# Feed-forward of a hybrid layer on one core: pools of their own for operands, weights and results, and the last pair's products stored by other queues

## The chip, the cores and the metric

The kernel runs on 1 core of one Trainium2 chip. The metric is the device time of one execution in microseconds (us), the median of the runs shown; lower is better. PE is TensorE, DVE VectorE, ACT ScalarE, POOL GpSimd, SP SyncE (it only issues transfers here); SPq is SP's queue of transfers.

## The reference

One layer: RMSNorm and an input projection, a Mamba-2 scan and differential attention side by side, an output projection, and the feed-forward, which is the part that matters here. All of it is float32, 1024 tokens by 1024 channels, with a feed-forward width of 2816.

```python
    x = x + jnp.concatenate([y_ssd, y_att], axis=-1) @ w_out[l]
    h = rms_norm(x, norm2_w[l])
    x = x + (jax.nn.silu(h @ w_gate[l]) * (h @ w_up[l])) @ w_down[l]
```

## The kernel before

Every float32 product is made of three matmuls (`mm3`, L168 to L170): each operand is split into a high part (a cast on ACT, L156) and a low remainder (a subtraction on DVE or POOL, L157).

**Gate and up.** The 2816 columns are 22 tiles `f` of 128. The first two go the plain way; the other 20 go through `GateUp`, one step per `f`, in which a 2x2 block scheme replaces eight block products by seven (`PRODUCTS`: a11, s2, s1, s3, a12, s4, a22, in this order). The activations' seven operands of four tiles each (`ops`) are made once and stay in SBUF, 16 KB a partition for each, seven in all; product `j` of each step reads only operand `PRODUCTS[j]`. A step is 7 x 4 x 3 = 84 matmuls into four PSUM banks a to d. The weights of a step come as four raw tiles `wr`, POOL makes four differences `t` of them (L1164), and ACT and DVE split the seven into `op`; `run` prepares step n+1 while step n multiplies. The result of step `f` is `m`, finished on DVE (L1216, L1233, L1238).

**The store of a pair.** After every second step `store_pair(i)` writes the seven operands that down needs of pair `i` to DRAM (`md[i]`): a11, a12, a22 straight from `m`, and s3, s1, s2, s4 after a POOL operation each (L1107, L1109, L1111, L1113) into `ss` and `sd`, which lie in the places of operand a21. All these stores, like nearly all loads, stand in SP's queue, in order.

**Down.** `CHUNKS` groups the 11 pairs as 3, 3, 3, 2. A chunk has four steps `Down(c, d)`, each with the same seven products: 7 x 3 x 3 = 63 matmuls (42 in the last chunk), 924 in all. `fetch_m` (L1279) loads a pair's product operand into `mr` and splits it into `mo`; 21 of these a chunk, used by its four steps. `Down.load` (L1294) fetches the weights `wr` of a step in one transfer; `Down.prepare` makes four temps on POOL (L1164) and splits seven operands (L1307 on ACT, L1308 on DVE). A product's result is added on DVE to `ua` or `acc` (L1326). `fetch_acc` loads `acc` (the residual) through POOL's queue. The last step of a chunk (`Ahead`) fetches the next chunk's operands.

**What sets the order around the change.** A scheduler places the instructions of each engine; a tile of a new pool waits for the last reader of whatever lay at its address. Before, the gate and up stage uses one pool `wg` for raw weights, temps, results and two of eight `op` places, and two pools `ra` and `rb` for the activations' operands, with tiles in the order in which they were asked for; down then opens `ac`, `wd`, `wde` on one side and one pool `rd` for the 24 `mo` tiles on the other. All seven stores of the last pair (pair 10, made by the last two steps) stand in SP's queue.

Of the kernel before, what the change touches and what calls it, by code (L numbers as in the profile page):

```python
# [7 lines left out]
F32 = mybir.dt.float32  # L8
F32R = mybir.dt.float32r
# [6 lines left out]
P = 128  # L16
# [58 lines left out]
def layer(ctx, tc, xT, wq0, wqkv, wxz, wout, wgu, wdn, pk, pb, cst, rot, sel, out):  # L75
# [841 lines left out]
    def split_y(src, kk, eng):  # L917
# [3 lines left out]
            res[hf] = split(place_of(tag).tile([P, S], F32R, tag=tag, name="y", bufs=4), src[:, 512 * hf : 512 * hf + 512], eng)  # L921
        return res

    def place_of(name):
        return rb if name in ("a11", "s2", "s1", "a12") else ra

    def fetch(dst, i):
        nc.sync.dma_start(out=dst, in_=yd[i])
# [7 lines left out]
    for u in range(2 * 4):  # L936
        g, p = divmod(u, 4)
        pair = Pair(g, p)
        if u > 0:
            flush()  # L940
        half()
        if prev:
            prev.gate()
        pair.tokens()
        pair.decay(0)
        if u == 4:
            group_rstd()
# [12 lines left out]
        pair.inside()  # L960
        if u == 4:
            for i in range(4):
                scale_y(0, i)
                nc.sync.dma_start(out=yd[i], in_=xg[(0, i)])
        half()
        pair.across()
        if u == 3:
            group_rows_dt(1)
            group(1)
        if u == 6:  # L970
            for i, b in ((0, 3), (1, 4), (2, 6), (3, 7)):
                yr[i] = fetch(big[b], 8 + i)
            assert not jobs
            xctx.close()
            rctx = ExitStack()
            ra = pool(rctx, "ra", side="right")
            pctx.close()
            psum[:] = [pool(pctx, "pso", bufs=2, space=PSUM), "mx"]
            for i in range(4):
                ys[i] = split_y(yr[i], i, V if i else G)  # L980
            for i, b in ((4, 3), (5, 4), (6, 6), (7, 7)):
                yr[i] = fetch(big[b], 8 + i)
            for q in range(2):
                for d in range(2):
                    add_out(d, 0, q)
            for q in range(2):
                add_out(2, 0, q)
            for d in range(3):
                add_out(d, 1, 0)
            add_last()  # L990
            for d in range(3, DK - NHALF):
                for hq in range(4):
                    add_out(d, hq // 2, hq % 2)
            for hf in range(2):
                for d in range(DK - NHALF, DK):
# [6 lines left out]
    del psum[1:]  # L1002
    half()
    s2ctx.close()
    rb = pool(rctx, "rb", side="right")
    for i, b in ((0, 3), (1, 4)):
        yr[i] = fetch(big[b], i)
    for i in range(2, 4):
# [88 lines left out]

    def store_pair(i):
        m0, m1 = ms.pop(2 * i), ms.pop(2 * i + 1)
        put = lambda name, t: nc.sync.dma_start(out=md[i][PRODUCTS.index(name)], in_=t)  # L1100
        for name, t, fs in (("a11", m0, halves[0]), ("a12", m1, halves[0]), ("a22", m1, halves[1])):
            put(name, t[:, fs])
        ss = ra.tile([P, S], F32, tag="a21", name="ss", bufs=4)
        s3, s1 = ss[:, 0:512], ss[:, 512:1024]
        sd = ra.tile([P, S], F32, tag="a21", name="sd", bufs=4)
# [44 lines left out]
    store_pair(0)  # L1150
    psum[0] = pool(ctx, "psm", bufs=2, space=PSUM)
    wg = pool(wbctx, "wg")


    class Weights:
# [27 lines left out]
    class GateUp:  # L1183
# [19 lines left out]

        def make(self, src):
            n = GateUp.slots[1] = (GateUp.slots[1] + 1) % 8
            op = wb[0].tile([P, S], F32R, tag="op", name="op", bufs=6) if n < 6 else wg.tile([P, S], F32R, tag="op", name="op", bufs=2)
            return split(op, src, V)

        def product(self, j):
            if j == 0:  # L1210
                self.ps = {b: psum[0].tile([P, 512], F32, tag=b, name="ps_" + b) for b in "abcd"}
            ps, w = self.ps[BANKS[j]], self.parts[j]
            for k in range(4):
                mm3(ps, w[:, k * P : (k + 1) * P], w[:, 512 + k * P : 512 + (k + 1) * P], ops[(PRODUCTS[j], k)], k == 0 and j < 4, k == 3, j > 3)
            tile_ = lambda: wg.tile([P, 512], F32, tag="u", name="u", bufs=4)
# [25 lines left out]
            if self.f % 2:  # L1241
                store_pair(self.f // 2)

    def run(steps):
        steps[0].load(range(4))
        for j in range(7):
            steps[0].prepare(j)
        if len(steps) > 1:
# [24 lines left out]
    mo = {}  # L1273

    def fetch_m(c, j):
        p0, n = CHUNKS[c]
        for i in range(n):
            mr = wde.tile([P, 512], F32, tag="mr", name="mr", bufs=6)
            nc.sync.dma_start(out=mr, in_=md[p0 + i][j])  # L1279
            mo[(c, j, i)] = split(rd.tile([P, S], F32R, tag="op", name="mo", bufs=24), mr, V)  # L1280

    class Down:
        slot = [-1]

        def __init__(self, c, d):
            self.c, self.d = c, d
# [3 lines left out]
        def load(self, which):  # L1290
            if 0 not in which:
                return
            wr = wd.tile([P, 3, 4, P], F32, tag="wr", name="wr", bufs=2)[:, : self.n]
            nc.sync.dma_start(out=wr, in_=wdn[self.p0 : self.p0 + self.n, self.d].rearrange("i p (q n) -> p i q n", n=P))  # L1294
            self.raw = [wr[:, :, q] for q in range(4)]

        def prepare(self, j):
            if j == 0:
                temp = lambda: wd.tile([P, 3, P], F32, tag="t", name="t", bufs=4)[:, : self.n]
                self.w = Weights(self.raw, temp, self.make)  # L1300
                self.parts = []
            self.parts.append(self.w.part(j))

        def make(self, src):
# [40 lines left out]


    wd.tile([P, 3, 4, P], F32, tag="wr", name="wr", bufs=2)
    wd.tile([P, 3, P], F32, tag="t", name="t", bufs=4)
    wd.tile([P, 2, 3, P], F32R, tag="op", name="op", bufs=4)
    wd.tile([P, 544], F32, name="pad1", bufs=1)  # L1350
    for j in range(7):
        fetch_m(0, j)
    fetch_acc(0)

    class Ahead(Down):

# [98 lines left out]
```

## Time and profile before

| what | us |
|---|---|
| median of 3 runs | 1685.81 (1684.41 to 1686.86) |
| the profiled execution's own time | 1682.61 |
| its span, first to last instruction | 1680.8 |
| PE busy in the span | 1623.5 (97%) |
| DVE busy | 1162.8 (69%) |
| ACT busy | 786.1 (47%) |
| POOL busy | 754.4 (45%) |
| granted TensorE clock, mean | 0.987 of full speed |

A busy share is an average over all stages. The page's second part cuts the span in 40 slices of 42 us; a slice in which PE is not at 9 is a place where PE waits, and the rows of windows and of the timeline show for what. The chain of waits goes back from the last instruction to what released it. The profiled execution is 3.2 us below the median of the runs.

### The profile page before, as it was taken

The page shows a single profiled execution, that of the slowest core. Times are in us where ns is not written, and L with a number is a line of the kernel's source. Part 1 is how long each engine was busy: PE and PEld are TensorE (multiplying, and loading weights), DVE is VectorE, ACT ScalarE, POOL GpSimd, SP SyncE. Part 2 cuts the span into 40 slices and gives each one's busy share as a digit, 9 for nine tenths or more (in the row PEclk, how much of TensorE's full clock was granted, in tenths as well). Part 3 has the DMA queues.
Part 4 walks back from the last instruction along what each step waited for, and adds up shares of the span by engine and source line. Part 5 has one row for each costly group of instructions (what it writes and reads, how often), then busy time and mean ns, then how long its engine had stood idle before and what let it go on. Part 6 is the DMA issues. An engine that isn't in the chain of part 4 may idle for free.

```text
span 1680.8 us, 23898 instructions
## 1 busy us (share of the span) xinstructions
PE 1623.5 (97%) x8237; PEld 1378.7 (82%) x8237; DVE 1162.8 (69%) x2217; ACT 786.1 (47%) x1759; POOL 754.4 (45%) x915
## 2 busy tenths in 40 slices
PE   7899999999999999999999998999999999699999
PEld 7799999999988778877778876788888888478887
DVE  7888788888887667786851258755555554499877
ACT  5576676666666454454532233333323332344531
POOL 5855665665441332343333328744443342433225
PEclk8899999999999999999999999999999999799999
DMA  5101110110011111131334321323223221755523
GB/s 188 38 17 36 51 36 21 47 48 11 20 64 32 51 38 38 39 137 45 107 116 155 118 82 54 128 104 112 98 101 107 100 101 51 265 183 178 180 78 113
DMA packets 78392, 146.50 MB, mean 87 GB/s; under 512 B 8490, under 2 KB 16938, under 8 KB 78272
## 3 DMA queue, kind: packets, MB, share of 16 engines
q1 hardware_dynamic: 66224, 131.21, 23.2%
q0 software_dynamic: 2544, 9.05, 1.5%
q10 hardware_dynamic: 9504, 4.72, 1.0%
q8 instruction: 65, 1.06, 0.3%
q14 instruction: 55, 0.45, 0.1%
HBM read 110.09 MB, written 34.87 MB: 86 GB/s over the span
## 4 chain that ended last, share of the span: by engine, by line
PE 85%; DVE 6%; ACT 3%; issue 3%; POOL 2%; DMA 1%; SPq 0%; DVEq 0%; ACTq 0%; POOLq 0%
PE ps_pj L207 5%; PE ps_pj L209 5%; PE ps_pj L208 5%; PE ps_x L485 5%; PE ps_x L486 4%; PE ps_x L487 4%; PE p L170 3%; PE p L168 3%; PE p L169 3%; PE ps_c L170 3%; PE ps_c L169 3%; PE ps_d L168 3%; PE ps_c L168 3%; PE ps_d L169 3%; PE ps_d L170 3%; PE ps_a L170 3%
## 5 line engine op out<-in xcount | busy, mean ns | idle before, releaser
L156 ACT CAST op<-wr 128x512 fp32r<-128x512 f32 x156 | 96.2, 618 | 258.2 <-PE ps_d L170 77.9
L157 DVE TENSOR_TENSOR op<-wr,op 128x512 fp32r<-128x512 f32 x108 | 89.6, 831 | 145.7 <-ACT op L156 142.9
L207 PE MATMUL ps_pj<-wh,xwh 128*128 128x384 f32 (+1 forms) x512 | 175.6, 347 | 7.0 <-ACT wh L150 6.2
L209 PE MATMUL ps_pj<-wh,xwl 128*128 128x384 f32 (+1 forms) x512 | 174.0, 342 | 3.2 <-DVE xwl L274 3.2
L1164 POOL TENSOR_TENSOR t<-wr,t 128x512 f32<-128x512 f32 (+2 forms) x72 | 93.3, 1296 | 183.6 <-issue 125.2
L208 PE MATMUL ps_pj<-wl,xwh 128*128 128x384 f32 (+1 forms) x512 | 174.3, 341 | 0.0
L157 POOL TENSOR_TENSOR op<-wr,op 128x512 fp32r<-128x512 f32 x48 | 64.4, 1343 | 211.3 <-ACT op L156 211.3
L1164 POOL TENSOR_TENSOR t<-wr 128x512 f32<-128x512 f32 (+2 forms) x72 | 89.3, 1240 | 104.1 <-DVE op L1308 55.6
L485 PE MATMUL ps_x<-xwh,op 128*128 128x512 f32 x320 | 129.7, 405 | 0.9 <-ACT ya L428 0.9
L486 PE MATMUL ps_x<-xwl,op 128*128 128x512 f32 x320 | 126.6, 396 | 0.0
L487 PE MATMUL ps_x<-xwh,op 128*128 128x512 f32 x320 | 126.4, 395 | 0.0
L382 ACT ACTIVATE pt<-ps_s,nm 128x640 f32<-128x640 f32 (+7 forms) x128 | 94.4, 741 | 44.4 <-DVE nm L377 24.3
L207 PEld LDWEIGHTS ps_pj<-wh,xwh 128*128 128x128 f32 x512 | 97.8, 191 | 7.6 <-ACT wh L150 7.3
L156 ACT CAST op<-t 128x512 fp32r<-128x512 f32 x80 | 49.6, 622 | 111.8 <-PE ps_c L170 55.5
L209 PEld LDWEIGHTS ps_pj<-wh,xwl 128*128 128x128 f32 x512 | 97.6, 191 | 3.9 <-DVE xwl L274 3.8
L169 PE MATMUL p<-y,op 128*128 128x512 f32 x256 | 100.8, 395 | 0.0
L170 PE MATMUL p<-y,op 128*128 128x512 f32 x256 | 100.7, 396 | 0.0
L168 PE MATMUL p<-y,op 128*128 128x512 f32 x256 | 99.0, 397 | 0.0
L157 DVE TENSOR_TENSOR op<-t,op 128x512 fp32r<-128x512 f32 x80 | 77.0, 965 | 31.6 <-ACT op L156 30.8
L208 PEld LDWEIGHTS ps_pj<-wl,xwh 128*128 128x128 f32 x512 | 97.8, 191 | 0.4
L377 DVE TENSOR_REDUCE nm<-ps_s 128x1 f32<-128x640 f32 (+7 forms) x128 | 93.7, 745 | 1.4
L410 PE MATMUL po<-v,wt 128*128 128x128 f32 x576 | 77.5, 276 | 0.0
(301 smaller groups left out, 4667.5 us busy)
## 6 DMA issues: line engine op xcount, KB each, us to landing
wr<-in_wgu_dram SPq DMA_DIRECT2D x88, 256.0 KB, 2.8
mr<-md SPq DMA_DIRECT2D x77, 256.0 KB, 3.2
wr<-in_wout_dram SPq DMA_DIRECT2D x48, 256.0 KB, 2.7
wr<-in_wqkv_dram SPq DMA_DIRECT2D x28, 384.0 KB, 3.1
wr<-in_wxz_dram SPq DMA_DIRECT2D x40, 256.0 KB, 2.8
wr<-in_wdn_dram SPq DMA_DIRECT2D x12, 768.0 KB, 4.6
md<-m SPq DMA_DIRECT2D x33, 256.0 KB, 2.0
md<-ss SPq DMA_DIRECT2D x22, 256.0 KB, 2.2
```

Of the source, the lines that this page charges most:

```text
L156: A.copy(out=op[:, 0:n], in_=src)
L157: eng.tensor_tensor(out=op[:, n : 2 * n], in0=src, in1=op[:, 0:n], op=ALU.subtract)
L168: T.matmul(out=ps, lhsT=wh, rhs=a[:, 0:512], start=first, stop=False, skip_group_check=more)
L169: T.matmul(out=ps, lhsT=wh, rhs=a[:, 512:1024], start=False, stop=False, skip_group_check=more)
L170: T.matmul(out=ps, lhsT=wl, rhs=a[:, 0:512], start=False, stop=last, skip_group_check=more)
L207: T.matmul(out=ps[:, :n], lhsT=xwh[k][:, ts], rhs=wh[:, k % 2, :], start=k == first, stop=False)
L208: T.matmul(out=ps[:, :n], lhsT=xwh[k][:, ts], rhs=wl[:, k % 2, :], start=False, stop=False)
L209: T.matmul(out=ps[:, :n], lhsT=xwl[k][:, ts], rhs=wh[:, k % 2, :], start=False, stop=k == last)
L485: T.matmul(out=ps, lhsT=wh[:, ks], rhs=xwh[k][:, fs], start=k == 0, stop=False)
L486: T.matmul(out=ps, lhsT=wh[:, ks], rhs=xwl[k][:, fs], start=False, stop=False)
L487: T.matmul(out=ps, lhsT=wl[:, ks], rhs=xwh[k][:, fs], start=False, stop=k == DK - 1)
L1164: G.tensor_tensor(out=self.t[name], in0=x, in1=y, op=ALU.subtract)
```

## The change

It gives each group of the feed-forward's tiles a pool of its own: every activation operand one (`open_parts`, in two orders: a21, s4, a22, s3, then a12, s1, s2, a11), raw weights and temps `wg`, results and spare operands `wu`; for down four pools on the left (`wd`, `wo`, `wd2`, `wo2`) behind `ac` and `ac2`, with pads, and six on the right (`rd[0]` to `rd[5]`), each of the size of one activation operand; `mo` tiles go round them in the order 5, 3, 4, 1, 2, 0. Of the last pair, a11, a12 and a22 are stored by ACT's queue, s1 to s4 by POOL's. The first weights of down are asked for ahead of the first operands. The arithmetic is the same, and so is the number of instructions of each kind but for these issues.

```diff
     def place_of(name):
-        return rb if name in ("a11", "s2", "s1", "a12") else ra
+        return parts[name]
+
+    def open_parts(*names):
+        for name in names:
+            parts[name] = pool(rctx, name, side="right")
...
-            ra = pool(rctx, "ra", side="right")
+            open_parts("a21", "s4", "a22", "s3")
...
-    rb = pool(rctx, "rb", side="right")
+    open_parts("a12", "s1", "s2", "a11")
...
-        put = lambda name, t: nc.sync.dma_start(out=md[i][PRODUCTS.index(name)], in_=t)
+
+        last = i == NPR - 1
+        put = lambda name, t: (nc.sync if not last else nc.gpsimd if name[0] == "s" else nc.scalar).dma_start(out=md[i][PRODUCTS.index(name)], in_=t)
...
-            op = wb[0].tile([P, S], F32R, tag="op", name="op", bufs=6) if n < 6 else wg.tile([P, S], F32R, tag="op", name="op", bufs=2)
+            op = wb[0].tile([P, S], F32R, tag="op", name="op", bufs=6) if n < 6 else wu.tile([P, S], F32R, tag="op", name="op", bufs=2)
...
-    acc = [ac.tile([P, S], F32, name=f"acc{d}") for d in range(DK)]
+    acc = [ac.tile([P, S], F32, name=f"acc{d}") for d in range(4)]
     ua = [ac.tile([P, 512], F32, name=f"ua{d}") for d in range(DK // 2)]
     ac.tile([P, S], F32, name="pad0")
+    ac2 = pool(ctx, "ac2")
+    acc += [ac2.tile([P, S], F32, name=f"acc{d}") for d in range(4, DK)]
     wd = pool(ctx, "wd")
-    wde = pool(ctx, "wde")
-    rd = pool(ctx, "rd", side="right")
+    wo = pool(ctx, "wo")
+    wd2 = pool(ctx, "wd2")
+    wo2 = pool(ctx, "wo2")
+    rd = [pool(ctx, f"rd{q}", side="right") for q in range(6)]
...
+    places = [(rd[q], n) for q in (5, 3, 4, 1, 2, 0) for n in range(4)]
...
+            n = Down.slot[1] = (Down.slot[1] + 1) % 4
+            return (wd2 if n < 2 else wd).tile([P, 3, P], F32, tag="t", name="t", bufs=2)[:, : self.n]
...
-            op = (wd if n > 5 else wde).tile([P, 2, 3, P], F32R, tag="op", name="op", bufs=4 if n > 5 else 6)[:, :, : self.n]
+            op = (wo2 if n < 5 else wo).tile([P, 2, 3, P], F32R, tag="op", name="op", bufs=5)[:, :, : self.n]
...
-    for j in range(7):
-        fetch_m(0, j)
-    fetch_acc(0)
...
-    run([(Ahead if d == DK // 2 - 1 else Down)(c, d) for c in range(len(CHUNKS)) for d in range(DK // 2)])
+    downs = [(Ahead if d == DK // 2 - 1 else Down)(c, d) for c in range(len(CHUNKS)) for d in range(DK // 2)]
+    downs[0].load(range(4))
+    for j in range(7):
+        fetch_m(0, j)
+    fetch_acc(0)
+    run(downs, loaded=True)
```

Up to the last gate and up step each engine's order is the same as before. SP's queue at the end of that step, before (`md` are the stores of a pair, `wr` the weights of down, `mr` its operands; md_93 is pair 9, md_94 the last pair):

```order
L1100 DMA md_93<-sd 128x512 x2
L1100 DMA md_94<-m 128x512
L1100 DMA md_94<-ss 128x512
L1279 DMA mr<-md_84 128x512
L1279 DMA mr<-md_85 128x512
L1279 DMA mr<-md_86 128x512
L1279 DMA mr<-md_84 128x512
L1279 DMA mr<-md_85 128x512
L1279 DMA mr<-md_86 128x512
L1100 DMA md_94<-m 128x512 x2
L1294 DMA wr<-in_wdn_dram 128x3x512 x2
L1100 DMA md_94<-ss 128x512
```

and in the change:

```order
L1109 DMA md_93<-sd 128x512 x2
L1316 DMA wr<-in_wdn_dram 128x3x512 x2
L1301 DMA mr<-md_84 128x512
L1301 DMA mr<-md_85 128x512
L1301 DMA mr<-md_86 128x512
L1301 DMA mr<-md_84 128x512
L1301 DMA mr<-md_85 128x512
L1301 DMA mr<-md_86 128x512
L1301 DMA mr<-md_84 128x512
```

The two weight loads now stand right behind pair 9's stores, and no store of the last pair stands among down's loads. PE at the same place, before (ps_d<-a is the seventh and last product of the last gate and up step, ps_a<-mo the first product of down):

```order
L168 MATMUL ps_d<-a_10653,op 128x512
L169 MATMUL ps_d<-a_10653,op 128x512
L170 MATMUL ps_d<-a_10653,op 128x512
L168 MATMUL ps_a<-mo,op 128x512
L169 MATMUL ps_a<-mo,op 128x512
```

and in the change (ps_c<-s is the sixth product):

```order
L170 MATMUL ps_c<-s_10877,op 128x512
L168 MATMUL ps_a<-mo,op 128x512
L169 MATMUL ps_a<-mo,op 128x512
L170 MATMUL ps_a<-mo,op 128x512
L168 MATMUL ps_a<-mo,op 128x512
L168 MATMUL ps_d<-a_10659,op 128x512
L169 MATMUL ps_d<-a_10659,op 128x512
```

Four matmuls of down now stand ahead of the last twelve of gate and up. ACT in the change, where before its casts of `mo` (L156) began only behind the last `gt` of gate and up (L1247 here is the silu of the last product, L1333 a cast of down's weights):

```order
L1333 CAST op<-wr 128x384
L1333 CAST op<-t 128x384 x3
L1333 CAST op<-wr 128x384
L156 CAST mo<-mr 128x512 x7
L1239 ACTIVATE gt<-ps_a 128x512
L156 CAST mo<-mr 128x512 x7
L1109 DMA md_94<-m 128x512
L156 CAST mo<-mr 128x512 x2
L1350 COPY ua_13969<-ps_a 128x512
L1333 CAST op<-t 128x384
L156 CAST mo<-mr 128x512
L1247 ACTIVATE gt<-gt 128x512
```

Sixteen casts of down's operands now stand ahead of that silu, and one of the last pair's stores among them.

## Rows read from the trace of the kernel before

**Rows 1.** The page's second part: PE's busy tenths and granted clock in 40 slices.

```profile
PE   7899999999999999999999998999999999699999
PEclk8899999999999999999999999999999999799999
```

**Rows 2.** PE's timeline: start, length (us), idle before and its releaser in brackets.

```profile
1440.83 0.40 PE L168 MATMUL ps_d<-a,op 128*128 128x512 f32 x1
...
1443.39 0.40 PE L170 MATMUL ps_d<-a,op 128*128 128x512 f32 x1
1452.13 0.80 PE L168 MATMUL ps_a<-mo,op 128*128 128x512 f32 x1 [8.34 <-ACT mo L156]
...
1457.66 0.79 PE L168 MATMUL ps_a<-mo,op 128*128 128x512 f32 x1 [3.26 <-ACT mo L156]
...
1667.51 0.39 PE L170 MATMUL ps_c<-mo,op 128*128 128x512 f32 x1
...
1676.47 0.39 PE L170 MATMUL ps_d<-mo,op 128*128 128x512 f32 x1
```

**Rows 3.** Windows: busy us (and count) of PE, PEld, DVE, ACT, POOL; clock; DMA share; GB/s.

```profile
1450.00:1460.00 10.00, 4.07 (x7) 2.15 (x8) 3.90 (x6) 3.73 (x7) 8.09 (x12) 0.50 1.01 376
1460.00:1470.00 10.00, 7.61 (x23) 5.24 (x23) 8.73 (x11) 7.41 (x16) 4.94 (x4) 0.71 1.03 402
...
1480.00:1490.00 10.00, 9.48 (x42) 7.28 (x41) 10.00 (x15) 5.16 (x12) 3.56 (x3) 1.00 0.64 229
...
1570.00:1580.00 10.00, 10.00 (x45) 8.22 (x44) 10.00 (x18) 7.29 (x15) 2.42 (x2) 1.00 0.79 242
```

**Rows 4.** The chain of waits between the two stages, in order of time.

```profile
1426.52 1.29 POOL ss L1107
1427.81 18.20 issue
...
1450.01 6.88 DMA md<-sd
1456.98 0.63 ACT mo L156
```

**Rows 5.** SP's queue: its timeline, then its longest wait of 1300 to 1500.

```profile
1409.70 2.03 SPq L1100 DMA_DIRECT2D md<-sd  x2
...
1442.60 3.71 SPq L1100 DMA_DIRECT2D md<-m  x2
1446.40 0.96 SPq L1294 DMA_DIRECT2D wr<-in_wdn_dram  x2
...
SPq L1100 <- DVE m L1233: 50.2, 8, 14.5
```

**Rows 6.** DVE's timeline in the last gate and up step.

```profile
1432.66 0.69 DVE L1216 TENSOR_TENSOR u<-ps_c,u 128x512 f32<-128x512 f32 x1 [2.02 <-PE ps_c L170]
```

**Rows 7.** Groups from 1440 to the end: busy us, mean ns | idle before.

```profile
L157 DVE TENSOR_TENSOR mo<-mr,mo 128x512 fp32r<-128x512 f32 x77 | 63.2, 849 | 5.4 <-ACT mo L156 5.4
L156 ACT CAST mo<-mr 128x512 fp32r<-128x512 f32 x77 | 46.2, 619 | 26.4 <-DMA mr<-md 20.4 <-DMA md<-sd 4.9 <-DMA wr<-in_wdn_dram 0.3
...
L1308 DVE TENSOR_TENSOR op<-t,op 128x384 fp32r<-128x384 f32 x48 | 30.0, 633 | 1.3 <-ACT op L1307 1.3
...
L1164 POOL TENSOR_TENSOR t<-wr,t 128x384 f32<-128x384 f32 x24 | 28.1, 1172 | 38.1 <-DVE op L1308 37.8
```

**Rows 8.** Transfers of `mr` from 1420 to 1500: issue to landing.

```profile
DMA to landing us min/median/max: 2.5/3.3/9.0
```

**Rows 9.** Windows of 4 us earlier, in the stage before gate and up.

```profile
1032.00:1036.00 4.00, 2.07 (x9) 1.37 (x8) 4.00 (x3) 2.33 (x6) 4.00 (x4) 0.96 0.25 75
1036.00:1040.00 4.00, 4.00 (x13) 3.09 (x11) 4.00 (x5) 2.35 (x4) 4.00 (x3) 0.61 0.16 58
...
1064.00:1068.00 4.00, 2.00 (x9) 1.35 (x8) 4.00 (x4) 2.14 (x4) 4.00 (x4) 1.00 0.72 238
```

**Rows 10.** Sum of the windows 1440, 1480, 1560, 1640 to 1681: busy us by engine.

```profile
sum 241.00, PE 221.81 PEld 178.12 DVE 195.87 ACT 96.20 POOL 92.99; mean PE 55.45 PEld 44.53 DVE 48.97 ACT 24.05 POOL 23.25
```

More of the change, by code (lines that the diff above doesn't have):

```diff
@@ L922, in split_y @@
         return res
+    parts = {}
     def place_of(name):
-        return rb if name in ("a11", "s2", "s1", "a12") else ra
+        return parts[name]
+    def open_parts(*names):
+        for name in names:
+            parts[name] = pool(rctx, name, side="right")
     def fetch(dst, i):
@@ L1099, in store_pair @@
         m0, m1 = ms.pop(2 * i), ms.pop(2 * i + 1)
-        put = lambda name, t: nc.sync.dma_start(out=md[i][PRODUCTS.index(name)], in_=t)
+        last = i == NPR - 1
+        put = lambda name, t: (nc.sync if not last else nc.gpsimd if name[0] == "s" else nc.scalar).dma_start(out=md[i][PRODUCTS.index(name)], in_=t)
         for name, t, fs in (("a11", m0, halves[0]), ("a12", m1, halves[0]), ("a22", m1, halves[1])):
             put(name, t[:, fs])
-        ss = ra.tile([P, S], F32, tag="a21", name="ss", bufs=4)
+        ss = parts["a21"].tile([P, S], F32, tag="a21", name="ss", bufs=4)
         s3, s1 = ss[:, 0:512], ss[:, 512:1024]
-        sd = ra.tile([P, S], F32, tag="a21", name="sd", bufs=4)
+        sd = parts["a21"].tile([P, S], F32, tag="a21", name="sd", bufs=4)
         s2, s4 = sd[:, 0:512], sd[:, 512:1024]
@@ L1152, in layer @@
     wg = pool(wbctx, "wg")
+    wu = pool(wbctx, "wu")
     class Weights:
@@ L1214, in product @@
                 mm3(ps, w[:, k * P : (k + 1) * P], w[:, 512 + k * P : 512 + (k + 1) * P], ops[(PRODUCTS[j], k)], k == 0 and j < 4, k == 3, j > 3)
-            tile_ = lambda: wg.tile([P, 512], F32, tag="u", name="u", bufs=4)
+            tile_ = lambda: wu.tile([P, 512], F32, tag="u", name="u", bufs=4)
             add = lambda o, x: V.tensor_tensor(out=o, in0=ps, in1=x, op=ALU.add)
@@ L1242, in end, with run @@
                 store_pair(self.f // 2)
-    def run(steps):
-        steps[0].load(range(4))
+    def run(steps, loaded=False):
+        if not loaded:
+            steps[0].load(range(4))
         for j in range(7):
@@ L1264, in layer, with mo_tile @@
     ac = pool(ctx, "ac")
-    acc = [ac.tile([P, S], F32, name=f"acc{d}") for d in range(DK)]
+    acc = [ac.tile([P, S], F32, name=f"acc{d}") for d in range(4)]
     ua = [ac.tile([P, 512], F32, name=f"ua{d}") for d in range(DK // 2)]
     ac.tile([P, S], F32, name="pad0")
+    ac2 = pool(ctx, "ac2")
+    acc += [ac2.tile([P, S], F32, name=f"acc{d}") for d in range(4, DK)]
     wd = pool(ctx, "wd")
-    wde = pool(ctx, "wde")
-    rd = pool(ctx, "rd", side="right")
+    wo = pool(ctx, "wo")
+    wd2 = pool(ctx, "wd2")
+    wo2 = pool(ctx, "wo2")
+    rd = [pool(ctx, f"rd{q}", side="right") for q in range(6)]
     mo = {}
+    places = [(rd[q], n) for q in (5, 3, 4, 1, 2, 0) for n in range(4)]
+    def mo_tile():
+        pl, n = places.pop(0)
+        places.append((pl, n))
+        return pl.tile([P, S], F32R, tag=f"op{n}", name="mo")
     def fetch_m(c, j):
@@ L1277, in fetch_m @@
         for i in range(n):
-            mr = wde.tile([P, 512], F32, tag="mr", name="mr", bufs=6)
+            mr = wd2.tile([P, 512], F32, tag="mr", name="mr", bufs=6)
             nc.sync.dma_start(out=mr, in_=md[p0 + i][j])
-            mo[(c, j, i)] = split(rd.tile([P, S], F32R, tag="op", name="mo", bufs=24), mr, V)
+            mo[(c, j, i)] = split(mo_tile(), mr, V)
     class Down:
-        slot = [-1]
+        slot = [-1, -1]
         def __init__(self, c, d):
@@ L1293, in load @@
             wr = wd.tile([P, 3, 4, P], F32, tag="wr", name="wr", bufs=2)[:, : self.n]
-            nc.sync.dma_start(out=wr, in_=wdn[self.p0 : self.p0 + self.n, self.d].rearrange("i p (q n) -> p i q n", n=P))
+            self.dma = nc.sync.dma_start(out=wr, in_=wdn[self.p0 : self.p0 + self.n, self.d].rearrange("i p (q n) -> p i q n", n=P))
             self.raw = [wr[:, :, q] for q in range(4)]
@@ L1298, in prepare @@
             if j == 0:
-                temp = lambda: wd.tile([P, 3, P], F32, tag="t", name="t", bufs=4)[:, : self.n]
+                temp = self.temp
                 self.w = Weights(self.raw, temp, self.make)
@@ L1302, in prepare, with temp @@
             self.parts.append(self.w.part(j))
+        def temp(self):
+            n = Down.slot[1] = (Down.slot[1] + 1) % 4
+            return (wd2 if n < 2 else wd).tile([P, 3, P], F32, tag="t", name="t", bufs=2)[:, : self.n]
         def make(self, src):
             n = Down.slot[0] = (Down.slot[0] + 1) % 10
-            op = (wd if n > 5 else wde).tile([P, 2, 3, P], F32R, tag="op", name="op", bufs=4 if n > 5 else 6)[:, :, : self.n]
+            op = (wo2 if n < 5 else wo).tile([P, 2, 3, P], F32R, tag="op", name="op", bufs=5)[:, :, : self.n]
             A.copy(out=op[:, 0], in_=src)
@@ L1347, in layer @@
     wd.tile([P, 3, 4, P], F32, tag="wr", name="wr", bufs=2)
-    wd.tile([P, 3, P], F32, tag="t", name="t", bufs=4)
-    wd.tile([P, 2, 3, P], F32R, tag="op", name="op", bufs=4)
-    wd.tile([P, 544], F32, name="pad1", bufs=1)
-    for j in range(7):
-        fetch_m(0, j)
-    fetch_acc(0)
+    wd.tile([P, 256], F32, name="pad1")
+    wd2.tile([P, 256], F32, name="pad2")
+    wo.tile([P, 288], F32, name="pad3")
     class Ahead(Down):
```

## The prediction

> **What bounds the kernel now.** I read the page's slices first. PE is at 9 nearly everywhere, so what a change can win lies in the few slices that are not; the one the change touches is the 35th, where PE falls to 6 tenths and the granted clock to 7 [rows 1]. It is the passage from gate and up to down. PE's timeline shows it from close by [rows 2]: the last matmul of gate and up starts at 1443.39, the first of down at 1452.13 after 8.34 us of waiting for a cast of `mo`, the next but two at 1457.66 after another 3.26. The windows show what follows [rows 3]: 7 matmuls from 1450 to 1460 at a clock of 0.50, 23 from 1460 to 1470 at 0.71, and 42 to 45 in ten us afterwards. 0.50 is the lower of the clock's two levels (1.2 GHz), and the engine had stood idle before it.
>
> What that costs in all: the last 40 matmuls start from 1667.51 to 1676.47 [rows 2], 8.96 / 39 = 0.230 us apart, which is the pace of a fed PE. Down has 924 matmuls. Without any loss the first would start at 1443.39 + 0.23 = 1443.62 and the last at 1443.62 + 923 x 0.230 = 1655.9. It starts at 1676.47. So **20.5 us** are lost after gate and up: 11.6 in the two named waits, the rest in half-clock matmuls and small gaps.
>
> Why: the chain of waits [rows 4] goes from POOL's `ss` at 1427.81 over an "issue" of 18.20 us to a store `md<-sd` of 6.88 us that lands at 1456.9, and only then is the next `mo` cast. The store matters because `ss` and `sd` lie where a `mo` tile is to be. SP's queue explains the 18 us [rows 5]: a store of the last pair stood at its head for 14.5 us, waiting for DVE's `m`, and all that follows it stood too, so that down's first weights were asked for at 1446.40 only.
>
> **The change, part by part.** Everything up to the last gate and up step keeps its order; all terms lie behind 1423.
>
> *Weights first.* Pair 9's stores leave SP at 1409.70 + 2.03 = 1411.7 [rows 5]. The `wr` loads come next instead of 35 us later, so they have landed long before use. The cost is two issues of 0.96 / 2 = 0.5 us on SP while nothing waits for it.
>
> *Seven stores leave SP.* SP loses seven issues; POOL gains four and ACT three, of about 0.5 us each by the same row. On POOL nothing of down waits behind them but temps and, later, `acc`; on ACT the two stores that wait for DVE's last `m` stand behind 14 and 19 casts of `mo`, and by my walk below DVE has made each `m` by the time that ACT is there. Pair 10 is read back by the last chunk alone, far later. I take nothing for them.
>
> *Places.* No `mo` tile waits for a store any more, except the ones laid over operand a21, which go last in the round of six; the others wait for the last reading of an activation operand, which comes product by product before 1443.
>
> *The walk.* POOL is free of `ss` at 1427.8 [rows 4]; two temps of 1.17 [rows 7] and a store's issue between them bring it to 1430.7. ACT casts weights and begins on `mo` by about 1433. DVE has its `u` done at 1432.66 + 0.69 = 1433.35 [rows 6], and then goes through four weight splits of 0.63, 21 `mo` splits of 0.85 [rows 7], and four gate and up results of 0.69 among them. PE wants the first `mo` at 1440.83, in the place that the first of the last twelve gate and up matmuls had [rows 2]; DVE has it at 1433.35 + 4 x 0.63 + 0.85 = 1436.7. That is 4.1 us of lead, so both named waits go, and with them the fall of the clock. The 15th tile is wanted 54 matmuls later, at 1453.2, and is ready at 1433.35 + 5 x 0.63 + 15 x 0.85 + 4 x 0.69 less one weight split that stands behind it = 1451.4: 1.8 ahead. This holds if `mr` keeps up: a load lands in 3.3 [rows 8], the cast takes 0.62 [rows 7], together 3.9, and the six buffers give six splits, 5.1 us, between asking and using. DVE sets the pace, not the transfers.
>
> *What stays lost.* First, the second step's operands. ACT makes them behind the 20th `mo`. The buffer of the 18th is free when the 12th split is done, at 1433.35 + 4 x 0.63 + 12 x 0.85 + 3 x 0.69 = 1448.1; landing at 1451.4; then eight casts and a store's issue on ACT, at 0.51 to 0.62 some 5 us, 1456.4. PE is there 66 matmuls behind 1440.83, at 1456.0. With a landing like the 6.88 of [rows 4] it is 1460.0. So 0 to 4.0 us; I take 1.0, near the lower end, since 3.3 is the median of these very loads. Second, the clock after such a gap. Between 1032 and 1036 PE was busy 2.07 of 4.00, and the clock went on at 0.96 and then 0.61 for four us; between 1064 and 1068 it was busy 2.00 of 4.00 and the clock stayed at 1.00 [rows 9]. The price by the first pair is 4 x 0.04 + 4 x 0.39 = 1.7, by the second nothing; I take 0.8. Third, DVE in the crowded first chunk. DVE was at 10.00 in both late windows of [rows 3]; in one PE had lost 3 matmuls, 0.7 us, in the other none. The change puts more of this next to PE at full speed: 0 to 5 us, of which I take 1.2, two such windows, rounded down.
>
> Together 3.0 us stay lost, between 0 and 10.7 at the two ends. The **gain** is 20.5 - 3.0 = 17.5. The profiled execution took 1682.6, so the changed one would take 1665.1. The median of the runs shown is 1685.8, 3.2 above that execution, and I add the 3.2: **1668.3 us**.
>
> **The rivals.** *Transfers bound the passage.* From 1450 to 1470 the 16 DMA engines were full, a share of 1.01 to 1.03 at 376 to 402 GB/s [rows 3], and a transfer took 6.88 [rows 4]. If `mr` takes that in the change too, a buffer's round is 6.88 + 0.62 + 0.85 = 8.35 instead of 5.1, 3.25 more for each of two rounds before the 15th tile: 6.5, less its lead of 1.8, makes a stall of 4.7. The clock then falls; the window with 23 matmuls where 43 fit lost 20 x 0.23 = 4.6, part of it in gaps, so 4.0. These 8.7 stand in place of the 1.8 of my first two terms: 9.9 stay lost, the gain is 10.6, the time 1675.2. Against it: the loads were crowded since stores, `wr`, `mr` and `acc` were all let go at once behind the 14.5 us wait, and the change spreads them over 40 us. The Trainium skill ("DMA: Bandwidth & Descriptors", section "Issuing engines are not separate DMA queues") says that transfers from the queues of several engines run on the same 16 DMA engines and interleave, and that issuing from several saves the time of issuing only. By that sentence the seven moved stores are worth 7 x 0.5 = 3.5 us and the time is about 1682; the row disagrees, since what stood in SP's queue was not a transfer but one wait of 14.5 us for DVE, with all the others behind it [rows 5].
>
> *DVE becomes the bound, and the kernel is slower.* DVE is busy 195.87 of the 241 us from 1440 to the end [rows 10]. Packed against an early PE, its operations may meet POOL's more often. From 1032 to 1036, with POOL busy all through, three DVE operations took 4.00 us, 1.33 each [rows 9] where one in gate and up took 0.69 [rows 6]. POOL is busy 92.99 us in down [rows 10], some 79 operations of 1.17. If each added 0.64 to one of DVE's, DVE would need 196 + 51 = 247 us from 1433.35 and end at 1680.3, where the kernel ends now; from there on it is slower. If two POOL operations in three cost DVE their whole length, it is 196 + 53 x 1.17 = 258, the end is 11 us later, and the time 1697. Against it: POOL's work stays the same in number, and in the window from 1570 eighteen DVE operations went through in 10.00 with PE full [rows 3]. The Trainium skill ("SBUF — State Buffer", section "SBUF: two separate sides") states that a GpSimd operation and a DVE one with two inputs in SBUF exclude each other on a shared pair of ports for a whole instruction. Splits of weights and `mo` are of that kind, so by it this rival's mechanism exists; the window from 1032 agrees, but nothing shows it two times in three.
>
> *The change doesn't do what it says.* If casts and splits still wait, now behind the in-order stores on ACT and POOL, or if places come free no earlier, PE waits as before and the time is 1685.8. Against it: 14 casts stand ahead of the first store that waits for the last `m`, more than PE needs in the first 10 us of down.
>
> **How the numbers follow.** My forecast has 0.79: its walk uses rows of these very operations, with leads of 4.1 and 1.8 us. Transfers bound 0.14, since the full engines are a fact and only their spreading is argued; no effect 0.03; slower 0.04. About 0.2%, 3.4 us, is what a measurement of this kernel can tell from no change. Forecast and first rival both lie beyond it, so faster is 0.93, same 0.03, slower 0.04. The range begins at 1664.5: with nothing left lost it would be 1685.8 - 20.5 = 1665.3, and 0.8 for the spread of runs. It ends at 1676.5, which takes in the transfers' case; the upper end of my own sum (a loss of 10.7) is 1676.0.
>
> **What would show it.** In the changed profile PE's windows from 1440 to 1470 should be at 10.00 with a clock of 1.00, but for a gap of a us or two near 1456; SP's rows should have `wr` at about 1412 and `mr` from 1425 on without a wait for `m`; the `md` stores of the last pair should stand on ACT's and POOL's queues; DVE should be nearly full from 1433 on; and the last matmul should start near 1659. I am wrong if a gap of over 4 us stands between 1441 and 1461 or the clock reads 0.50 there (then the transfers, if `mr` takes 6 us to land), or if DVE is at 10.00 for long with PE well under 43 matmuls in ten us (then DVE).

## The result, and the profile after

The changed kernel takes **1676.61 us** in the median of 5 runs (1671.85 to 1678.74), the kernel before 1685.81 beside it; the ratio is 0.9941, with a 95% interval of 0.9927 to 0.9954. It is faster, by 9.2 us between the medians and not by the 17.5 that I had worked out, and it lies 0.1 above the end of the range that I gave (1676.5).

The page's second part, with PE's busy tenths and clock, answers to [rows 1]:

```profile
PE   7899999999999999999999998899999999999999
PEclk9899999999999999999999999999999999999999
```

The 35th slice is at 9 for both. The hole is gone as a slice, but not all of it, as PE's timeline shows (start, length, idle before and its releaser; [rows 2] before):

```profile
1444.89 0.40 PE L168 MATMUL ps_a<-mo,op 128*128 128x512 f32 x1
...
1458.42 0.50 PE L168 MATMUL ps_a<-mo,op 128*128 128x512 f32 x1 [1.33 <-ACT ua L1350]
...
1464.50 0.50 PE L168 MATMUL ps_a<-mo,op 128*128 128x512 f32 x1 [1.70 <-ACT op L1333]
...
1469.57 0.50 PE L168 MATMUL ps_c<-mo,op 128*128 128x512 f32 x1 [3.41 <-DVE acc L1352]
...
1660.32 0.39 PE L170 MATMUL ps_b<-mo,op 128*128 128x512 f32 x1
...
1669.38 0.39 PE L168 MATMUL ps_d<-mo,op 128*128 128x512 f32 x1
...
1670.52 0.39 PE L170 MATMUL ps_d<-mo,op 128*128 128x512 f32 x1
```

Down's first matmul has no wait: the 8.34 and the 3.26 of before are gone. Three smaller waits have come: for ACT, for ACT again, and for DVE. And the row at 1669.38 is the 40th behind 1660.32: 9.06 / 40 = 0.2265 (0.2267 from longer stretches). That is the pace of a fed PE now, where it was 0.230 before.

The windows (busy us and count of PE, PEld, DVE, ACT, POOL; clock, DMA share, GB/s; [rows 3] before):

```profile
1450.00:1460.00 10.00, 8.36 (x34) 5.78 (x33) 7.58 (x13) 6.91 (x12) 0.08 (x1) 1.00 0.95 322
1460.00:1470.00 10.00, 4.89 (x21) 3.40 (x20) 10.00 (x12) 4.97 (x11) 8.44 (x10) 1.00 0.80 265
1470.00:1480.00 10.00, 10.00 (x39) 8.02 (x38) 4.34 (x8) 0.59 (x1) 0.90 (x2) 0.83 0.92 338
```

PE is at 4.89 from 1460 to 1470 while DVE is full with 12 operations only, and in the first of these windows ACT and DVE have time to spare: ACT waits for transfers, and DVE for ACT.

SP's queue, which had its first weights at 1446.40 in [rows 5], and DVE's first `mo` splits:

```profile
1415.73 11.57 SPq L1316 DMA_DIRECT2D wr<-in_wdn_dram  x2
1428.98 39.80 SPq L1301 DMA_DIRECT2D mr<-md  x26
```

```profile
1440.00 2.93 DVE L157 TENSOR_TENSOR mo<-mr,mo 128x512 fp32r<-128x512 f32 x2
```

Of the 11.57, 10.7 are a wait at the head of SP's queue, until DVE has done with the place of the second load of `wr`; the loads of `mr` follow at 1428.98.

**One ruler for both.** From the slot of down's first matmul to its last it is 1676.47 - 1440.83 = 235.6 us before and 1670.52 - 1444.89 = 225.6 now, 935 intervals in both (twelve matmuls of gate and up lie among them). At 0.2267 us they would take 212.0. So 23.7 were lost before by this ruler, and 13.7 are lost now: 10.0 won. The profiled execution took 1676.89, 5.7 less than that of before, and not 10.0, because its down began 4.06 later: 2.4 of this came before gate and up, where the two kernels do the same, and 1.6 in gate and up, whose matmuls stood 0.2333 us apart instead of 0.2324.

### The profile page after: what moved, and what is told of

It is laid out like the page before. It is cut to its first block, busy times and chain, and to the rows that moved or that the text cites. A ratio compares the mean times of both kernels' runs of the same rounds, so it can differ in the third digit from the quotient of the medians.

```text
span 1675.1 us, 23895 instructions
## 1 busy us (share of the span) xinstructions
PE 1623.0 (97%) x8237; PEld 1377.5 (82%) x8237; DVE 1163.3 (69%) x2217; ACT 786.0 (47%) x1759; POOL 756.8 (45%) x919
## 4 chain that ended last, share of the span: by engine, by line
PE 79%; DVE 9%; issue 3%; DMA 3%; POOL 3%; ACT 2%; SPq 0%; DVEq 0%; ACTq 0%; POOLq 0%
PE ps_pj L209 5%; PE ps_pj L207 5%; PE ps_pj L208 5%; PE ps_x L485 5%; PE ps_x L486 4%; PE ps_x L487 4%; PE ps_c L168 3%; PE ps_d L169 3%; PE ps_d L170 3%; PE ps_d L168 3%; PE ps_c L169 3%; PE ps_c L170 3%; PE p L170 3%; PE p L168 3%; PE po L410 3%
## 5 line engine op out<-in xcount | busy, mean ns | idle before, releaser
L156 ACT CAST op<-wr 128x512 fp32r<-128x512 f32 x156 | 96.3, 619 | 260.4 <-PE ps_d L170 78.2
L156 ACT CAST op<-t 128x512 fp32r<-128x512 f32 x80 | 49.6, 622 | 112.6 <-PE ps_c L170 56.0
```

The source lines that it names most:

```text
L156: A.copy(out=op[:, 0:n], in_=src)
```

## The experiments

Twelve kernels, each beside runs of the kernel before on the same chip; the ratios are against that.

### Which part of the change carries it

e1 puts all stores back on SP's queue, and keeps the rest:

```diff
-        put = lambda name, t: (nc.sync if not last else nc.gpsimd if name[0] == "s" else nc.scalar).dma_start(out=md[i][PRODUCTS.index(name)], in_=t)
+        put = lambda name, t: nc.sync.dma_start(out=md[i][PRODUCTS.index(name)], in_=t)
```

> The change with one part undone: all seven stores of the last pair stand in SP's queue again; pools and weights-first stay. Theory (places carry the gain, the queues little): the scheduler can now place two stores that wait for the last m behind 15 and 18 loads of mr, so PE still has its first mo before 1445, no wait of over 4 us at the passage, and the time is 0 to 4 us above the change's 1676.6, 1677 to 1681. Rival (the 14.5 us at the head of SP's queue were the cause): SP stands again for 8 us or more, PE waits over 5 us near 1448, time 1683 or more.

Measured: 1668.06 us, ratio 0.9896 (0.9880 to 0.9913). That is 8.5 us *faster* than the change, better than the theory's own forecast. SP never stood long for DVE's `m` again (SP's waits from 1425 to 1475: in all, times, longest):

```profile
SPq L1109 <- DVE m L1248: 1.1, 1, 1.1
```

With the old pools that was 14.5 in [rows 5]. The scheduler now puts loads ahead of such a store. That it can because their places come free sooner is my reading; no run tests it.

e2 is the opposite: the kernel before, with the other queues for the last pair and the weights asked for first, and its old pools:

```diff
+        last = i == NPR - 1
-        put = lambda name, t: nc.sync.dma_start(out=md[i][PRODUCTS.index(name)], in_=t)
+        put = lambda name, t: (nc.sync if not last else nc.gpsimd if name[0] == "s" else nc.scalar).dma_start(out=md[i][PRODUCTS.index(name)], in_=t)
...
+    downs[0].load(range(4))
     for j in range(7):
         fetch_m(0, j)
```

> The kernel before with two parts of the change alone: the last pair stored by ACT's and POOL's queues, and down's first weights asked for ahead of the operands; pools as before. Theory (places carry the gain): ACT's casts of mo still begin only when the last gate and up results are done, so PE waits 4 to 7 us between the stages and the clock still falls; gain 2 to 6 us, time 1680 to 1684. Rival (the queue carries it): no wait over 2 us, time 1677 or less.

Measured: 1686.13, ratio 1.0007 (0.9998 to 1.0016): no gain at all, less than both expected. PE's timeline, ACT's and POOL's show why:

```profile
1458.83 0.80 PE L168 MATMUL ps_a<-mo,op 128*128 128x512 f32 x1 [12.24 <-ACT mo L156]
```

```profile
1455.97 1.46 ACT L1309 CAST op<-t 128x384 fp32r<-128x384 f32 x3 [6.29 <-POOL t L1165]
...
1458.16 0.61 ACT L156 CAST mo<-mr 128x512 fp32r<-128x512 f32 x1
1459.18 2.70 ACT L156 CAST mo<-mr 128x512 fp32r<-128x512 f32 x5 [0.40 <-DMA md<-sd]
```

```profile
1450.99 1.27 POOL L1112 TENSOR_TENSOR sd<-ss,m 128x512 f32<-128x512 f32 x1
1452.21 1.00 POOL L1165 TENSOR_TENSOR t<-wr 128x384 f32<-128x384 f32 x1
```

In the kernel before, ACT's first cast of `mo` at 1451.46 (the 8.34 us of [rows 2]) stood right behind a cast of weights that had waited for `wr`:

```profile
1451.04 0.51 ACT L1307 CAST op<-wr 128x384 fp32r<-128x384 f32 x1 [5.80 <-DMA wr<-in_wdn_dram]
```

In e2 the weights are asked for at 1431.50, and that wait is gone. But now the first cast of `mo` stands behind casts of POOL's temps, and POOL makes these from 1452.21 on, among the sums of the last pair. In the change it makes all but one of them from 1431.75 to 1442.38, ahead of the last three of those sums. The second cast of `mo` still waits for the store of `sd`, over whose place its tile lies, but by 0.40 us only. So with the old pools PE waits for another part of the same order, whichever queue takes the stores. **Without the new pools there is no gain; the moved stores carry none of it.** Two things are not separated: weights-first stands in e1 and e2 alike, so it gains nothing alone and its share beside the pools is open; and no run has the new pools for `mo` without those for temps and weights.

e6 (the first added line) and e7 (the second) move the stores back by halves:

```diff
-        put = lambda name, t: (nc.sync if not last else nc.gpsimd if name[0] == "s" else nc.scalar).dma_start(out=md[i][PRODUCTS.index(name)], in_=t)
+        put = lambda name, t: (nc.sync if not last or name[0] == "s" else nc.scalar).dma_start(out=md[i][PRODUCTS.index(name)], in_=t)
...
+        put = lambda name, t: (nc.sync if not last or name[0] == "a" else nc.gpsimd).dma_start(out=md[i][PRODUCTS.index(name)], in_=t)
```

> The change with s1 to s4 of the last pair stored by SP again, a11, a12 and a22 still by ACT. Theory (the four stores on POOL's queue are what cost the change 8 us against all stores on SP: they stand between POOL's sums, push the second half of acc and the temps back, and with them DVE): time 1667 to 1671. Rival (the three on ACT are what costs): 1674 to 1679.

> The change with a11, a12 and a22 of the last pair stored by SP again, s1 to s4 still by POOL. Theory (the four on POOL cost): time 1674 to 1679. Rival (the three on ACT cost): 1667 to 1671.

Measured: 1669.18 (0.9893 to 0.9925) and 1670.55 (0.9904 to 0.9934). Both are as fast as e1, so neither half alone is what costs: my pair of theories was the wrong one. In each of these three kernels the scheduler also laid the passage's instructions in another order, PE's among them, and so they do not say which single instruction costs the 8 us. What they have in common is less lost at the passage by the ruler above: 8.4, 6.8 and 9.4 us instead of 13.7; another 1.6 is the pace of gate and up, which stays open below. For the causes I took kernels whose order stays, or nearly.

### The transfers: acc in the middle of mr

In the change POOL issues four loads of `acc`, 2 MB, at 1442.33, just as the second round of `mr` is wanted. ACT's waits from 1425 to 1475, and the landing of `mr` from 1420 to 1470 ([rows 8] before had a median of 3.3):

```profile
ACT mo L156 <- DMA mr<-md: 11.8, 7, 4.2
```

```profile
DMA to landing us min/median/max: 2.7/4.3/8.5
```

The chain of waits holds the worst one, and later a load of weights:

```profile
1445.40 8.33 DMA mr<-md
...
1468.98 11.64 DMA wr<-in_wdn_dram
```

e5 issues `acc` from SP's queue, behind the 21 loads of `mr`; on PE only two runs of matmuls in the second step change places:

```diff
-            nc.sync.dma_start(out=mr, in_=md[p0 + i][j])
+            gate[0] = nc.sync.dma_start(out=mr, in_=md[p0 + i][j])
...
-            nc.gpsimd.dma_start(out=acc[d], in_=x2d[d])
+            with tc.issue_after(gate[0].ins):
+                nc.sync.dma_start(out=acc[d], in_=x2d[d])
```

> The change with one part moved: the loads of acc (4 of 512 KB, then 4 more) go by SP's queue, behind the 21 loads of mr, instead of by POOL's queue in the middle of them; hardly anything else in the orders moves. Theory (acc's 2 MB crowd the mr loads, which land in 4.3 us at the median and 8.5 at the worst, where I took 3.3): landing of mr falls to 3.5 us or less, the waits and short delays of PE from 1453 to 1459 (2.4 us) go, time 1672 to 1674.5; the 3.4 us wait for ps_c near 1466 stays. Rival (mr loads are slow by themselves): landing stays over 4 us, time 1675 to 1678.

Measured: 1669.16, ratio 0.9912 (0.9897 to 0.9927), 7.4 below the change. ACT's wait for `mr`, the windows and all of PE's waits from 1420 to the end:

```profile
ACT mo L156 <- DMA mr<-md: 7.0, 6, 4.1
```

```profile
1450.00:1460.00 10.00, 10.00 (x46) 8.27 (x45) 10.00 (x15) 9.16 (x19) 3.56 (x3) 1.00 0.97 334
1460.00:1470.00 10.00, 6.03 (x20) 4.48 (x19) 8.53 (x12) 1.47 (x4) 3.71 (x5) 0.83 1.02 390
```

```profile
PE ps_a L170 <- DVE op L1336: 4.0, 1, 4.0
```

The waits for ACT are gone, and so are those that the change had later, near 1489, 1514 and 1532, which I had not connected with `acc`: the weights of the third and fourth step landed in 8.5 us here (median of two) and in 12.6 in the change, so that POOL made their temps at 1472 and not at 1481, and DVE had less to make up. Lost by the ruler: 6.0. The engines were no less full (0.97 and 1.02), and the median landing of `mr` hardly fell (4.2), against my expectation. That median hides what changed. The six loads asked for from 1442.6 to 1447, which PE needs next, landed so in the change and then in e5:

```profile
DMA to landing us min/median/max: 5.1/8.2/8.5
```

```profile
DMA to landing us min/median/max: 2.7/3.5/4.5
```

In e5 the slow ones, 8.3 to 10.3 us, are the five loads behind `acc`, and PE waits for none of them. What is left is one wait, for DVE.

### DVE against POOL's sums

In e5 DVE's and POOL's timelines at that wait read:

```profile
1457.93 1.65 DVE L1336 TENSOR_TENSOR op<-wr,op 128x384 fp32r<-128x384 f32 x1
1459.50 0.68 DVE L157 TENSOR_TENSOR mo<-mr,mo 128x512 fp32r<-128x512 f32 x1
1460.11 1.80 DVE L157 TENSOR_TENSOR mo<-mr,mo 128x512 fp32r<-128x512 f32 x1
1461.83 2.09 DVE L1336 TENSOR_TENSOR op<-wr,op 128x384 fp32r<-128x384 f32 x1
1463.84 0.54 DVE L1336 TENSOR_TENSOR op<-wr,op 128x384 fp32r<-128x384 f32 x1
```

```profile
1457.48 1.68 POOL L1118 TENSOR_TENSOR ss<-m 128x512 f32<-128x512 f32 x1 [0.63 <-DVE m L1248]
...
1460.04 1.31 POOL L1120 TENSOR_TENSOR sd<-ss,m 128x512 f32<-128x512 f32 x1
...
1462.22 1.27 POOL L1122 TENSOR_TENSOR sd<-m,sd 128x512 f32<-128x512 f32 x1
```

Three of these five DVE operations meet a sum of the last pair. They take 1.65, 1.80 and 2.09 us, and each ends 0.42 to 0.56 behind the end of its sum, a little less than its own length; the two that meet none take 0.68 and 0.54. (The 1.2 and 1.28 in the expectation below are means of a long and a short one.) Together the five take 6.5 us. In the change itself three splits meet the three sums in the same way, just before PE's wait of 3.41 ends, and take 1.63 and then:

```profile
1464.35 1.93 DVE L157 TENSOR_TENSOR mo<-mr,mo 128x512 fp32r<-128x512 f32 x1
1466.21 2.23 DVE L157 TENSOR_TENSOR mo<-mr,mo 128x512 fp32r<-128x512 f32 x1
```

e9 gives these three sums to DVE:

```diff
-        G.tensor_tensor(out=s1, in0=m0[:, 512:1024], in1=m1[:, 512:1024], op=ALU.add)
+        E = V if last else G
+        E.tensor_tensor(out=s1, in0=m0[:, 512:1024], in1=m1[:, 512:1024], op=ALU.add)
...
-        G.tensor_tensor(out=s2, in0=s1, in1=m0[:, 0:512], op=ALU.subtract)
+        E.tensor_tensor(out=s2, in0=s1, in1=m0[:, 0:512], op=ALU.subtract)
...
-        G.tensor_tensor(out=s4, in0=m1[:, 0:512], in1=s2, op=ALU.subtract)
+        E.tensor_tensor(out=s4, in0=m1[:, 0:512], in1=s2, op=ALU.subtract)
```

> The kernel with acc on SP's queue, and of the last pair the sums s1, s2 and s4 made by DVE instead of POOL. There DVE's operations beside POOL's three sums took 1.65, 1.2, 1.2, 1.28 and 1.28 us and alone take 0.55 to 0.68, about 3.3 us too much, and PE waited 4.0 for the last of them. Theory (the sums and DVE's operations hold each other up): only one sum of 0.69 stands ahead of what PE waits for, the wait falls to 1 to 2 us, the operations there take 0.55 to 0.7, time 1665.5 to 1668 against 1669.2. Rival (DVE's own load): the wait is 4.0 to 4.7, time 1669 to 1671.

Measured: 1667.90, ratio 0.9900 (0.9884 to 0.9917), which can't be told from e5 by the time alone. The mechanism can be told: DVE's rows there, and PE's waits to the end:

```profile
1454.90 0.55 DVE L1337 TENSOR_TENSOR op<-wr,op 128x384 fp32r<-128x384 f32 x1
1455.37 1.28 DVE L157 TENSOR_TENSOR mo<-mr,mo 128x512 fp32r<-128x512 f32 x2
1456.58 0.68 DVE L1119 TENSOR_TENSOR ss<-m 128x512 f32<-128x512 f32 x1
1457.18 1.01 DVE L1337 TENSOR_TENSOR op<-wr,op 128x384 fp32r<-128x384 f32 x2
```

```profile
PE ps_d L169 <- DVE mo L157: 1.2, 1, 1.2
PE ps_c L168 <- DVE acc L1355: 1.2, 2, 0.8
PE ps_a L170 <- DVE op L1337: 1.1, 2, 0.9
```

The five operations and the sum between them take 3.3 us where the five alone took 6.5, and that sum takes 0.68 where POOL needed 1.68. The wait of 4.0 fell to 0.9. The waits of 1.2 and of 0.8 and less are new, at 1479, 1502 and 1519, so that 5.6 are lost by the ruler instead of 6.0. PE's order differs too, in the second step and behind it; e11 below is the closer test. The Trainium skill ("SBUF — State Buffer", section "SBUF: two separate sides") has a GpSimd operation and a DVE operation with two inputs in SBUF exclude each other for whole instructions; these rows agree with it, 1.65 to 2.09 us beside a sum and 0.54 to 0.68 without one. The operation of 2.09 us began 0.39 ahead of its sum and still ended behind it; POOL was issuing a store when it began, and no run separates that issue from the sum.

### The pace of the matmuls

Why is down's pace 0.2267 now and 0.230 before, and gate and up's 0.2333? The built programs give the addresses. In the change all ten of down's weight places start at 224 modulo 256 bytes, and so do its operands `mo`. Before, four of the ten started at 96, and in gate and up all do, in both kernels. The kernel before shows both within down: behind 1480 its matmuls start 0.2275 us apart where the weights stand at 224 (487 intervals) and 0.2327 where they stand at 96 (305). e3 takes 128 bytes from down's last pad, and moves no instruction:

```diff
-    wo.tile([P, 288], F32, name="pad3")
+    wo.tile([P, 256], F32, name="pad3")
```

> The change with its last pad 128 bytes shorter, so that down's weight places start at 96 modulo 256 bytes and its operands at 224, as in gate and up; every engine's order stays as it is. Theory (matmuls are some ns slower when weights and moving operand stand 128 bytes apart modulo 256): down's pace goes from 0.2267 to about 0.2325 us for each of 924 matmuls, the time is 4 to 6 us above the change's, 1680.5 to 1682.5; gate and up stay at 0.2333. Rival (the pace comes from what else runs): pace stays at 0.2267, time within 1.5 us of 1676.6.

Measured: 1678.21, ratio 0.9959 (0.9947 to 0.9971). Forty intervals of PE in down:

```profile
1659.80 0.41 PE L169 MATMUL ps_a<-mo,op 128*128 128x512 f32 x1
...
1669.10 0.39 PE L170 MATMUL ps_c<-mo,op 128*128 128x512 f32 x1
```

9.30 / 40 = 0.2325, as the theory had it. The time rose by 1.6 only and not by 4 to 6: by the ruler 17.6 are lost instead of 13.7, 3.9 more, as a slower PE waits a little less for DVE; the rest is within what the runs of the change spread by (7 us). The pace decides it. e4 goes the other way, with 128 bytes under the weight places of the output projection and of gate and up, and down's left side moved along:

```diff
-            wb.append(pool(wbctx, "wb"))
+            wb.append(pool(wbctx, "wb")); wb[0].tile([P, 32], F32, name="padw")
...
-    ac = pool(ctx, "ac")
+    ac = pool(ctx, "ac"); ac.tile([P, 32], F32, name="padw")
...
...
-    wo.tile([P, 288], F32, name="pad3")
+    wo.tile([P, 256], F32, name="pad3")
```

> The change with 128 bytes put under all weight places of output projection and gate and up (and down's left side moved along, its own weights where they were); every engine's order stays as it is. Theory (alignment sets the pace): gate and up go from 0.2333 to 0.2268 us a matmul, 1680 x 0.0065 = 11 us less, and the plain part and the output projection (1150 matmuls, 0.231 to 0.227) up to 4 more; time 1661 to 1667. Rival (the pace comes from what else runs): no change, 1675 to 1678.

Measured: **1660.14**, ratio 0.9853 (0.9839 to 0.9868), 16.5 below the change and 0.9 below the forecast's range. In gate and up, forty intervals of the change and forty of e4:

```profile
1299.75 0.40 PE L170 MATMUL ps_d<-s,op 128*128 128x512 f32 x1
...
1309.09 0.40 PE L168 MATMUL ps_d<-a,op 128*128 128x512 f32 x1
```

```profile
1299.62 0.39 PE L170 MATMUL ps_a<-a,op 128*128 128x512 f32 x1
...
1308.68 0.39 PE L168 MATMUL ps_a<-a,op 128*128 128x512 f32 x1
```

0.2335 and 0.2265 us each. e12 moves down's weights and operands both to 128 modulo 256:

```diff
+    rpad = pool(ctx, "rpad", side="right"); rpad.tile([P, 24], F32, name="padr")
     rd = [pool(ctx, f"rd{q}", side="right") for q in range(6)]
...
-    wo.tile([P, 288], F32, name="pad3")
+    wo.tile([P, 264], F32, name="pad3")
```

> The change with down's operands and weights both moved to 128 modulo 256 bytes (each mo place now reaches into two old places, so the passage gets slower; only the pace is of interest). Theory (what counts is the distance of the two modulo 256, which is 0 again): down's matmuls start 0.2267 us apart as in the change. Rival (what counts is where each stands): a pace that differs by 0.002 us or more.

```profile
1649.68 0.39 PE L169 MATMUL ps_a<-mo,op 128*128 128x512 f32 x1
...
1658.75 0.39 PE L170 MATMUL ps_a<-mo,op 128*128 128x512 f32 x1
```

9.07 / 40 = 0.2267: two operands at the same place modulo 256 bytes are as fast at 128 as at 224. One rival is left, that weights at 96 are slow wherever the moving operand stands: no matmul here of 512 columns has both at 96, or the weights at 224 and the moving operand at 96. The input projection has the latter with 384 columns, 0.176 us a matmul against 0.174 with both at 224 (some 540 and 610 intervals of the change): a hint that the distance counts, but a smaller loss, and not a test. e12's one run took 1667.85, faster than the change, though I had expected a slower passage; it lost 7.6 by the ruler, in another order again.

### The parts together

e8 is e1 with e4's 128 bytes; e10 is e8 with e5's `acc`; e11 is e10 with e9's sums.

> All stores on SP's queue together with the 128 bytes under the weight places of output projection and gate and up. If the two are independent: 1668.1 less 16.5, so 1650 to 1654, faster than every kernel so far. Rival (with PE faster, DVE and the transfers bound the passage and take part of it back): 1655 to 1660.

> Three parts together: all stores on SP's queue, acc on SP's queue behind mr, 128 bytes under the weight places of output projection and gate and up. If they add up: 1669.2 less 16.5, 1650.5 to 1653.5, below the 1654.0 without acc's move. Rival (SP's queue now holds stores, mr and acc in order and one of them waits): 1654 to 1658.

> The kernel of e10 with s1, s2 and s4 of the last pair made by DVE. Theory as for e9: 1.5 to 3 us below e10, 1648 to 1651. Rival: equal to e10 or up to 2 us above.

Measured: 1654.02 (ratio 0.9818, 0.9802 to 0.9835), 1651.35 (0.9803, 0.9787 to 0.9820) and **1646.81** (0.9775, 0.9760 to 0.9789). e11 is the fastest, 38 us below the kernel before and 30 below the change, and lower than its forecast. PE's only wait from 1415 to the end, in e10 and then in e11:

```profile
PE ps_a L170 <- DVE op L1336: 2.7, 1, 2.7
```

```profile
PE ps_a L170 <- DVE op L1337: 0.6, 1, 0.6
```

By the ruler e11 loses 1.0 us where the kernel before lost 23.7. The sums on DVE are worth 4.5 us here between the medians (1651.35 and 1646.81); by the ruler 2.0 of it lie in down (3.0 lost in e10, 1.0 in e11), and where the rest lies I did not find. ACT's order is the same in both and PE's differs in one exchange of six matmuls with six. e10 against e8 is the cleanest test of `acc`, since PE, DVE and ACT have the same order in both: 2.7 us between the medians, less than the 7.4 of e5.

## Why the prediction was right, and where it was not

**What held.** The hole was there because of the old places and the order that they bring, and new places close it: e1 closes it with the stores on SP's queue, e2 with the old pools does not. Of the two named waits, the place under `sd` accounts for the second, 3.26; the first, 8.34, came from weights asked for late, as I had read it from SP's queue. But e2 asks for them early and gains nothing, since with the old pools POOL's temps hold PE there instead. The walk held as far as its first lead: I had the first `mo` ready 4.1 us ahead of PE, and it was 1444.89 - 1440.00 - 2.93 / 2 = 3.4 ahead. Both named waits went, and the clock stayed at 1.00 to 1470. The first weights went out at 1415 and had landed long before use. That the moved stores are worth nothing, as I had them in the sum, e2 shows (ratio 1.0007); in the change as built they did not pay either, as e1 without them is 8.5 us faster. The sentence of the Trainium skill that I weighed there ("DMA: Bandwidth & Descriptors", section "Issuing engines are not separate DMA queues") was right on this one point, with even the 3.5 us of issuing not to be seen; the 1682 that I drew from it was wrong, since the gain lies in the places.

**The step that failed is "what stays lost".** The sign that I had named for DVE came from 1460 to 1470: DVE at 10.00 with 21 matmuls on PE. I had 3.0 us; it is 13.7 by the ruler, or 10.6 if the faster pace is counted against it (935 x (0.2300 - 0.2267) = 3.1), and 20.5 - 10.6 = 9.9, the 10 us that were won. Term by term, from the idle and slow intervals of PE (0.4 more is spread over the rest):

- *The second step's operands*, 1.0 in the sum: 2.0 at 1464.50, and 2.6 before it between 1453 and 1459. I took 3.3 for a landing because it was the median of these loads before; now single loads took up to 8.5, with `acc`'s 2 MB among them. The row with 6.88, the full engines of [rows 3] and the worst landing of [rows 8], 9.0, were the better guide. I had argued that the change spreads the transfers, and had not looked where POOL's queue would put `acc`: right behind its temps, now earlier than PE's need of `mr`. e5 shows this term: with `acc` moved it goes, and the later waits for DVE go with it.
- *DVE in the crowded first chunk*, 1.2 in the sum: 3.7 at 1469.57 and 3.4 from 1481 to 1533. The 3.7 is POOL's three sums beside DVE's splits, which took 1.63, 1.93 and 2.23 us instead of 0.55 to 0.68. I had the price (1.33 instead of 0.69 in [rows 9]) in a rival that needed it everywhere; it needed to happen once, where PE waited. e9 and e11 show it.
- *The clock*, 0.8 in the sum: 1.6, the price that [rows 9] gave for its first pair.
- *The pace*, taken as 0.230 before and after: 0.2267, 3.1 us in favour. A diff that moves pools and adds pads of 288 and 256 words moves addresses, and I had no term for addresses. e3, e4 and e12 show what they are worth. That the result came so near the end of my range is luck by this much: e3, the change without the faster pace, took 1678.21.

The first rival, that transfers bound the passage, gave 1675.2, the nearest number of all, in part by luck: it had 4.7 for the stall, 4.0 for the clock, which took 1.6, and 1.2 for DVE, for which PE waited 7.1. Its stall by `mr` was the larger part of what was lost (4.6 at once and 3.4 later, all gone in e5), but not the whole, as 5.3 belong to DVE, POOL and the clock.

**What stays open.** Gate and up ran at 0.2333 in the change, e3 and e12 and at 0.2324 in e1, e2, e5, e6, e7 and e9, with the same addresses and the same order of instructions there (and at 0.2324 in the kernel before); 1.6 us, not explained. And which part of the new order makes e1, e6 and e7 faster than the change was not separated.

## What to carry to other kernels

When a hole between two stages is closed, ask at once what each queue will issue in the new gap: a transfer that nobody needs for 25 us can take the engines from one that is needed now, and moving it behind was worth 7.4 us here, and 2.7 in another order. Two engines that work on SBUF side by side may hold each other up, so look which of POOL's operations stand beside the DVE operation that PE waits for. And read addresses as part of a diff of pools: 128 bytes under the weight places were worth 16.5 us.

## What the runs showed of the hardware

I had not expected that a matmul's pace depends on where weights and moving operand stand: with 128 rows, 512 columns, float32r and a fed PE at a clock of 1.00, 0.2267 us where both start at the same place modulo 256 bytes (224 or 128), and 0.2324 to 0.2335 where they stand 128 bytes apart (weights at 96, moving operand at 224). Other distances, and both at 96, were not tried. That DVE's splits and POOL's operations hold each other up I had seen in the trace of before (1.33 us for 0.69); new is how closely a split waits for a sum to end, 1.65 to 2.09 us instead of 0.54 to 0.68, and that PE would wait 3.4 us for it.
